# Hybrid diffusion backbone: the scan's decay matrices built in whole rows, and an instruction order taken from the timing simulator

## The chip, the cores and the metric

The kernel runs on one core of a Trainium2 chip. The metric is device time in microseconds (us) of one execution. TensorE (PE) does matmuls and, on a second track (PEld), loads their weights; VectorE (DVE), ScalarE (ACT) and GpSimd (POOL) do the rest; SyncE (SP) and POOL issue most of the transfers (DMA) between memory (HBM) and on-chip SBUF. Every engine takes its own instructions strictly in the order in which the program lists them, and waits on semaphores for the others.

## The reference

Two layers (`DEPTH = 2`) over 256 latent and 256 context tokens of width 1024. A layer is a token mixer with three branches (HGRN2 linear recurrence, grouped-query attention, Mamba-2 SSD), then a SwiGLU network. The last layer computes outputs for latent tokens alone. The change is in the SSD branch: 4 groups of 8 heads, scanned forward and backward in chunks of 128 tokens.

```python
def step(state, blk):                      # ssd_scan, one chunk
    xc, dtc, bc, cc = blk
    acum = jnp.cumsum(dtc * a, axis=1)
    seg = acum[:, :, None, :] - acum[:, None, :, :]
    decay = jnp.exp(jnp.where(causal, seg, -jnp.inf)).reshape(n, L, L, G, HPG)
    xdt = (xc * dtc[..., None]).reshape(n, L, G, HPG, MB_HEAD_DIM)
    cb = jnp.einsum("btgn,bsgn->btsg", cc, bc)
    y = jnp.einsum("btsg,btsgh,bsghp->btghp", cb, decay, xdt)
    ...                                    # plus C against the carried state
```

For each head the kernel needs a matrix over (s, t) of exp(acum_t - acum_s), cut to a triangle, times the step size of s, times C·B. Forward and backward are summed before the matmul.

## The kernel before

**Dense products.** Weights are streamed in pieces of 512 KB by SP (`Weights._load`) into 4 buffers `wraw`. `_split` (L125, L126) makes of each piece a rounded part `wh` on ACT and a remainder `wl` on DVE, with 3 buffers each; a dense product is three matmuls (`mm3`: hh·wh, hl·wh, hh·wl) into a PSUM tile `g`. 48 such matmuls make a unit. The adaLN weights come as "ticks" (`mod_step`): a piece of 512 KB that is not split, read by 8 matmuls `mod` right out of `wraw`, with a tick behind each unit.

**Staging.** Each layer runs the SSD branch, then HGRN2, attention, merge, output projection and feed-forward. `Weave` mixes two generators in the order in which they are recorded: dense units as the main one, the branch's own steps as the side one. In the SSD stage the side one is `ssd_scan` for one group: transposes `xtok`, `Btok`, `cb` = C·B, `state`, and then four pairs of heads. At a layer's start `ssd_tok` transposes the step sizes (`dtT`).

**One head before.** POOL loads the head's cumulated decay row for both directions to all partitions (`ab`, 512 KB) from a DRAM tile `sd`, and e^acum (`ce`, 256 KB) from the same tile. `tk` holds log(dt_s) - acum_s, one number to a partition. DVE makes D = ab + tk + triangle (`neg`) for every 128x128 block and direction; ACT takes exp of D as a whole, and separately exp of the blocks that need no triangle into M; DVE adds the two directions in M and multiplies by `cb`. Then PE does the pair's `y` matmuls from M and from `ce`. In layer 0 a head has both token segments (1024 columns), in layer 1 the latent one alone (512).

**Buffers.** `ab`, D, M, `xt`, `cb`, `state` and others share 10 buffers "b" of 128x1032; 53 buffers "a" of 128x512 hold `ce` and everything else. A load into a buffer waits until the last reader of its old contents is done.

**Order.** Within data dependencies a scheduler in the tile framework sets each engine's order: it plays the recorded program on a model of the machine and issues what is ready there, by priority. Buffers are given out in the same run.

Of the kernel before, what the change touches and what calls it, by code (L numbers as in the profile page):

```python
# [6 lines left out]
F32 = mybir.dt.float32  # L7
F32R = mybir.dt.float32r
I32 = mybir.dt.int32
AF = mybir.ActivationFunctionType  # L10
ALU = mybir.AluOpType
AX = mybir.AxisListType.X

P = 128
# [4 lines left out]
SEQ = 256  # L19
CTX = 256  # L20
T = SEQ + CTX
# [17 lines left out]
def vw(ap, off, dims):  # L39
    return bass.AP(ap.tensor, ap.offset + off, [list(ap.ap[0])] + [list(d) for d in dims])  # L40
# [103 lines left out]
class Net:  # L144
# [468 lines left out]
        yield  # L613


    def ssd_dt_plan(self, l):
        self.w.add(("dt", l), [self.io["w_in"][l][:, O_DT:O_DT + 64].rearrange("(k p) c -> p k c", p=P)])

    def ssd_dt(self, l):

        nc, lay = self.nc, self.lay[l]
        R, N = 64, SEQ
        wh, wl = self.w.take(("dt", l))
        ps = self.pg()
        for k in range(ND):
            self.mm3(ps[0:R, :], wh[:, k], wl[:, k], self.hh[k], self.hl[k], k == 0, k == ND - 1)
        self.act(lay["a"], self.par(l, V_AL), AF.Exp)
        self.ts(lay["a"], lay["a"], -1.0, ALU.mult)
        x, m, y, r, z, p = (self.a(name=n)[:, 0:N] for n in ("dx", "dm", "dy", "dr", "dz", "dp"))
        for sg in range(2):  # L630
            self.ts(x[R * sg:R * sg + R], ps[0:R, N * sg:N * sg + N], self.par(l, V_DTB)[0:R], ALU.add)
        self.ts(m, x, 0.0, ALU.max)
        self.act(y, x, AF.Abs)
        self.act(y, y, AF.Exp, scale=-1.0)
        self.ts(r, y, 2.0, ALU.add)
        nc.vector.reciprocal(out=r, in_=r)
        self.tt(z, y, r, ALU.mult)
        self.tt(z, z, z, ALU.mult)
        self.ts(p, z, 1.0 / 15.0, ALU.mult)
        for c in (13, 11, 9, 7, 5, 3):  # L640
            self.stt(p, p, 1.0 / c, z, ALU.add, ALU.mult)
        self.ts(r, r, 2.0, ALU.mult)
        self.stt(r, p, 1.0, r, ALU.add, ALU.mult)
        dt = z
        self.tt(dt, y, r, ALU.mult)
        self.tt(dt, dt, m, ALU.add)
        self.act(y, m, AF.Exp, scale=-1.0)
        self.tt(y, y, r, ALU.mult)
        self.tt(y, y, m, ALU.add)
        self.act(y, y, AF.Ln)  # L650
        ln = r
        self.stt(ln, x, 0.0, y, ALU.min, ALU.add)
        da, one, s = p, m, x
        self.ts(da, dt, lay["a"], ALU.mult)
        nc.vector.memset(one, 1.0)
        for sg in range(2):
            f, b = slice(R * sg, R * sg + 32), slice(R * sg + 32, R * sg + R)
            nc.vector.tensor_tensor_scan(out=s[f], data0=one[f], data1=da[f], initial=0.0, op0=ALU.mult, op1=ALU.add)
            rv = lambda t: vw(t[b], N - 1, [[-1, N]])
            nc.vector.tensor_tensor_scan(out=rv(s), data0=one[b], data1=rv(da), initial=0.0, op0=ALU.mult, op1=ALU.add)  # L660
        sd = self.dp.tile([R, T + SEQ], F32, name=f"sd{l}")
        for sg in range(2):
            nc.gpsimd.dma_start(out=sd[:, N * sg:N * sg + N], in_=s[R * sg:R * sg + R])
        es = one
        self.act(es[R:P], s[R:P], AF.Exp)
        nc.gpsimd.dma_start(out=sd[:, T:T + SEQ], in_=es[R:P])
        pt = y
        self.tt(pt, ln, s, ALU.subtract)
        we = z
        self.ts(we[0:32], pt[0:32], s[0:32, N - 1:N], ALU.add)  # L670
        self.ts(we[32:R], pt[32:R], s[32:R, 0:1], ALU.add)
        self.last = self.act(we[0:R], we[0:R], AF.Exp)
        return {"sd": sd, "pt": pt, "we": we}
# [89 lines left out]

    def ssd_scan(self, l, g, st, dts, wc, ys):

        nc, lay = self.nc, self.lay[l]
        if "tk" not in dts:
            self.ssd_tok(dts)
        sd, tk = dts["sd"], dts["tk"]
        ts = T + SEQ  # L770
        q0 = 0 if wc else CTX
        segs = (0, 1) if wc else (1,)
        s0, ns = segs[0], len(segs)
        xt, bt = [self.b(name="xt") for _ in range(2)], self.a(name="bt")
        xs = lambda tt, o, n: xt[tt // 2][:, 512 * (tt % 2) + o:512 * (tt % 2) + o + n]
        for tt in range(4):
            ps = self.ps("xtok")
# [4 lines left out]
        ps = self.ps("Btok")  # L782
# [4 lines left out]
        cb = self.b(name="cb")  # L787
        for sg in segs:
            ps = self.ps("cb")
            for s in range(2):  # L790
                c = 256 * sg
                self.mm(ps[:, 256 * s:256 * s + 256], st["B"][:, c + P * s:c + P * s + P], st["C"][:, c:c + 256])
            self.act(cb[:, 512 * sg:512 * sg + 512], ps, AF.Copy)
        yield
        state = self.b(name="state")
        for dr in range(2):
            ps = self.ps("state")
# [7 lines left out]
        for pr in range(4):  # L805
            ms, ce = {}, {}
            for i in range(2):
                h = 8 * g + 2 * pr + i
                ab = self.b(name="ab")
                nc.gpsimd.dma_start(out=ab.rearrange("p (d t) -> p d t", d=2),  # L810
                                    in_=bass.AP(sd.tensor, sd.offset + h * ts, [[0, P], [32 * ts, 2], [1, T]]))
                D, M = self.b(name="D"), self.b(name="M")
                for sg in segs:
                    for s in range(2):
                        tt = 2 * sg + s
                        for dr in range(2):
                            o = 512 * sg + 256 * s + P * dr
                            self.stt(D[:, o:o + P], ab[:, T * dr + P * tt:T * dr + P * tt + P],
                                     tk[:, tt, 32 * dr + h:32 * dr + h + 1], self.neg[:, dr, :], ALU.add, ALU.add)
                        o, a0 = 512 * sg + 256 * s + P * (1 - s), T * s + 256 * sg + P * (1 - s)  # L820
                        self.act(M[:, o:o + P], ab[:, a0:a0 + P], AF.Exp, bias=tk[:, tt, 32 * s + h:32 * s + h + 1])
                dv = D[:, 512 * s0:1024]
                self.last = self.act(dv, dv, AF.Exp)
                o = 512 * s0
                self.tt(vw(M, o, [[512, ns], [256 + P, 2], [1, P]]), vw(D, o, [[512, ns], [256, 2], [1, P]]),
                        vw(D, o + P, [[512, ns], [256, 2], [1, P]]), ALU.add)
                self.tt(M[:, o:1024], M[:, o:1024], cb[:, o:1024], ALU.mult)
                ms[i] = M
                e = self.a(name="ce")
                ev = e.rearrange("p (d t) -> p d t", d=2)  # L830
                nc.gpsimd.dma_start(out=ev, in_=bass.AP(sd.tensor, sd.offset + h * ts + T, [[0, P], [32 * ts, 2], [1, SEQ]]))
                self.tt(ev, ev, vw(st["C"], CTX, [[0, 2], [1, SEQ]]), ALU.mult)
                ce[i] = e
                yield
            yp = self.ps("y")
            for sg in segs:
                ops = [[], []]
                for i in range(2):
                    hc = 64 * (2 * pr + i)
                    ops[i] += [(xs(2 * sg + s, hc, 64), ms[i][:, 512 * sg + 256 * s:512 * sg + 256 * s + 256]) for s in range(2)]  # L840
                    if sg == 1:
                        ops[i] += [(state[:, 512 * dr + hc:512 * dr + hc + 64], ce[i][:, SEQ * dr:SEQ * dr + SEQ]) for dr in range(2)]
                n = len(ops[0])
                for j in range(n):
                    for i in range(2):
                        self.mm(yp[64 * i:64 * i + 64, 256 * sg:256 * sg + 256], *ops[i][j], j == 0, j == n - 1)
            y = self.a(name="y")
            n = 4 * g + pr
            self.stt(y[:, q0:T], st["x"][pr][:, q0:T], self.par(l, V_D + n), yp[:, q0:T], ALU.mult, ALU.add)
            ys.append(y)  # L850
            yield
# [732 lines left out]
```

## Time and profile before

| | us |
|---|---|
| median of 3 runs (lowest, highest) | 2683.18 (2682.48, 2686.78) |
| profiled execution, its own time | 2682.9 |
| its span, first to last instruction | 2681.0 |
| PE busy | 2597.5 (97%) |
| DVE, ACT, POOL busy | 1782.2, 1233.2, 193.0 |
| mean DMA rate | 139 GB/s over the span |

The profiled execution is 0.3 us below the median. PE is busy almost throughout, so the table alone says little: the ends of matmuls are modelled and overlap, a busy PE can run at half clock, and the waits lie in a few stages. The stages of the profiled execution are: the start to 40 us (adaLN weights), layer 0's SSD to 536 us, its HGRN2 to 1206, the rest of layer 0 to 1675, layer 1's SSD to 2010, its HGRN2 to 2300, then attention, merge and feed-forward to the end.

### The profile page before, as it was taken

How to read it: one execution, taken by the hardware profiler on the slowest of the kernel's cores; microseconds unless marked ns; L12 is line 12 of the kernel's file. 1: busy time of each engine (PE TensorE's matmuls, PEld its weight loads, DVE VectorE, ACT ScalarE, POOL GpSimd, SP SyncE). 2: the span in 40 equal slices, each digit the busy share in tenths (PEclk: the TensorE clock that was granted, in tenths of full speed). 3: DMA queues.
4: the chain of work that ended last, by engine and by line, in shares of the span. 5: the costliest groups of instructions: out<-in, count | busy, mean ns of one | idle time of the engine just before them, and what ended most of it. 6: DMA issues, size and time to landing. Idle time of an engine off the chain costs nothing. (4 is left out here: it accounts for less than half of the span.)

```text
span 2681.0 us, 46307 instructions
## 1 busy us (share of the span) xinstructions
PE 2597.5 (97%) x18660; PEld 2139.5 (80%) x18660; DVE 1782.2 (66%) x3708; ACT 1233.2 (46%) x2030; POOL 193.0 (7%) x320
## 2 busy tenths in 40 slices
PE   7999989999999999999999999899999999999999
PEld 4767667788888897777888878677878898888998
DVE  5887776756565575457533358887877777857555
ACT  3655554632333324545432226565654334465543
POOL 0111010000000001010000000111110011111000
PEclk9999999999999999999999999899999999999999
DMA  7566555544444444352333323455763353446553
GB/s 248 147 178 178 147 163 157 150 120 116 118 142 134 123 138 154 94 194 70 102 95 102 95 79 99 132 161 161 222 185 108 98 144 109 140 122 201 166 183 109
DMA packets 298952, 374.41 MB, mean 140 GB/s; under 512 B 16433, under 2 KB 251985, under 8 KB 298737
## 3 DMA queue, kind: packets, MB, share of 16 engines
q1 hardware_dynamic: 271568, 284.21, 35.2%
q0 software_dynamic: 25728, 84.61, 11.1%
q8 instruction: 147, 2.41, 0.4%
q10 hardware_dynamic: 1440, 2.62, 0.3%
q14 instruction: 69, 0.56, 0.1%
HBM read 355.27 MB, written 16.12 MB: 139 GB/s over the span
## 5 line engine op out<-in xcount | busy, mean ns | idle before, releaser
L126 DVE TENSOR_TENSOR wl<-wraw,wh 128x1024 fp32r<-128x1024 f32 (+1 forms) x450 | 544.0, 1211 | 417.1 <-ACT wh L125 408.6
L125 ACT ACTIVATE wh<-wraw 128x1024 fp32r<-128x1024 f32 (+1 forms) x450 | 470.9, 1048 | 699.1 <-PE g L204 509.9
L204 PE MATMUL g<-hh,wh 128*128 128x512 f32 (+2 forms) x2032 | 731.8, 362 | 4.8 <-ACT hh L190 2.2
L204 PE MATMUL g<-hh,wl 128*128 128x512 f32 (+2 forms) x2032 | 723.0, 357 | 5.3 <-DVE wl L126 5.3
L204 PE MATMUL g<-hl,wh 128*128 128x512 f32 (+2 forms) x2032 | 724.6, 357 | 0.0
L204 PEld LDWEIGHTS g<-hh,wh 128*128 128x128 f32 (+1 forms) x2032 | 386.5, 191 | 75.9 <-issue 15.5
L204 PEld LDWEIGHTS g<-hh,wl 128*128 128x128 f32 (+1 forms) x2032 | 386.8, 191 | 68.7 <-issue 9.5
L204 PEld LDWEIGHTS g<-hl,wh 128*128 128x128 f32 (+1 forms) x2032 | 387.4, 191 | 61.8 <-issue 12.9
L204 PE MATMUL g<-oh,wh 128*128 128x512 f32 (+1 forms) x864 | 300.9, 350 | 2.4 <-DVE gl L193 1.3
L204 PE MATMUL g<-ol,wh 128*128 128x512 f32 (+1 forms) x864 | 295.3, 342 | 0.2 <-DVE ol L196 0.2
L204 PE MATMUL g<-oh,wl 128*128 128x512 f32 (+1 forms) x864 | 292.8, 340 | 0.5 <-DVE wl L126 0.5
L204 PE MATMUL g<-wh,hh 128*128 128x256 f32 x768 | 220.7, 287 | 0.0
L204 PE MATMUL g<-wh,hl 128*128 128x256 f32 x768 | 219.2, 285 | 0.0
L204 PE MATMUL g<-wl,hh 128*128 128x256 f32 x768 | 218.1, 284 | 0.0
L204 PEld LDWEIGHTS g<-oh,wh 128*128 128x128 f32 x864 | 163.7, 190 | 29.6 <-issue 7.9
L204 PEld LDWEIGHTS g<-ol,wh 128*128 128x128 f32 x864 | 164.3, 190 | 22.7 <-issue 6.3
L204 PEld LDWEIGHTS g<-oh,wl 128*128 128x128 f32 x864 | 164.0, 190 | 20.2 <-issue 2.7
L204 PEld LDWEIGHTS g<-wh,hh 128*128 128x128 f32 x768 | 147.1, 192 | 3.1 <-issue 2.6
L204 PEld LDWEIGHTS g<-wh,hl 128*128 128x128 f32 x768 | 147.2, 192 | 2.2 <-issue 1.9
L204 PEld LDWEIGHTS g<-wl,hh 128*128 128x128 f32 x768 | 147.2, 192 | 0.5 <-issue 0.4
L196 DVE SCALAR_TENSOR_TENSOR u<-craw,vec,u 128x508 f32<-128x508 f32 (+3 forms) x192 | 130.6, 721 | 8.6 <-ACT u L190 7.6
L196 DVE SCALAR_TENSOR_TENSOR D<-ab,tk,neg 128x128 f32<-128x128 f32 x384 | 110.2, 346 | 22.3 <-DMA ab<-sd 22.1
(303 smaller groups left out, 3577.7 us busy)
## 6 DMA issues: line engine op xcount, KB each, us to landing
wraw<-in_w_in SPq DMA_DIRECT2D x216, 512.0 KB, 4.1
wraw<-in_w_mod SPq DMA_DIRECT2D x96, 512.0 KB, 4.1
wraw<-in_w_ffn_in SPq DMA_DIRECT2D x88, 512.0 KB, 3.5
ab<-sd POOLq DMA_DIRECT2D x64, 512.0 KB, 6.8
wraw<-in_w_ffn_out SPq DMA_DIRECT2D x40, 512.0 KB, 3.4
ce<-sd POOLq DMA_DIRECT2D x64, 256.0 KB, 7.6
wraw<-in_w_br_mb SPq DMA_DIRECT2D x32, 512.0 KB, 3.4
wraw<-in_w_in SPq DMA_DIRECT2D x34, 256.0 KB, 3.6
```

The costliest lines, as they stand in the source:

```text
L125: self.nc.scalar.activation(hi[:, 0:n], t[:, 0:n], AF.Copy)
L126: self.nc.vector.tensor_tensor(out=lo[:, 0:n], in0=t[:, 0:n], in1=hi[:, 0:n], op=ALU.subtract)
L196: return self.nc.vector.scalar_tensor_tensor(out=out, in0=a, scalar=s, in1=b, op0=op0, op1=op1)
L204: return self.nc.tensor.matmul(out, l, r, start=start, stop=stop)
```

## The change

`sd` gets 256 more columns: per direction and segment a copy of the 128 positions whose block needs the other direction's triangle. A head now loads M itself from the decay rows (direction by direction, all positions of its segments), and a small tile E (from the 53 buffers "a") with the other direction's rows of the diagonal blocks. DVE adds the triangles to the diagonal blocks of M in one instruction and to E in another; ACT takes exp in place with `tk` as its per-partition bias (256 columns at a time in M, 128 in E); DVE adds E into M's diagonal blocks and multiplies by `cb`. D and `ab` are gone. `cb` and the `y` matmuls follow M's new layout (s outermost). The scheduler's model is exchanged for the timing simulator by one argument.

```diff
@@ ssd_dt
-        sd = self.dp.tile([R, T + SEQ], F32, name=f"sd{l}")
+        sd = self.dp.tile([R, self.SD], F32, name=f"sd{l}")       # SD = T + SEQ + 2 * P
         for sg in range(2):
             nc.gpsimd.dma_start(out=sd[:, N * sg:N * sg + N], in_=s[R * sg:R * sg + R])
+            for d in range(2):
+                o, r = T + SEQ + P * sg, 32 * d
+                nc.gpsimd.dma_start(out=sd[r:r + 32, o:o + P], in_=s[R * sg + r:R * sg + r + 32, P * (1 - d):P * (1 - d) + P])
@@ ssd_scan, one head
-                ab = self.b(name="ab")
-                nc.gpsimd.dma_start(out=ab.rearrange("p (d t) -> p d t", d=2),
-                                    in_=bass.AP(sd.tensor, sd.offset + h * ts, [[0, P], [32 * ts, 2], [1, T]]))
-                D, M = self.b(name="D"), self.b(name="M")
+                M, E = self.b(name="M"), self.a(name="E")
+                whole = lambda z: vw(z, 256 * s0, [[512, 2], [1, 256 * ns]])
+                diag = vw(M, 256 * s0, [[512 + P, 2], [256, ns], [1, P]])
+                other = vw(E, P * s0, [[256, 2], [P, ns], [1, P]])
+                row = sd.offset + h * ts + 256 * s0
+                nc.gpsimd.dma_start(out=whole(M), in_=bass.AP(sd.tensor, row, [[0, P], [32 * ts, 2], [1, 256 * ns]]))
+                nc.gpsimd.dma_start(out=vw(E, P * s0, [[256, 2], [1, P * ns]]),
+                                    in_=bass.AP(sd.tensor, row + T + SEQ - P * s0, [[0, P], [32 * ts, 2], [1, P * ns]]))
+                for z in (diag, other):
+                    self.tt(z, z, vw(self.neg, 0, [[P, 2], [0, ns], [1, P]]), ALU.add)
                 for sg in segs:
                     for s in range(2):
-                        tt = 2 * sg + s
-                        for dr in range(2):
-                            o = 512 * sg + 256 * s + P * dr
-                            self.stt(D[:, o:o + P], ab[:, T * dr + P * tt:T * dr + P * tt + P],
-                                     tk[:, tt, 32 * dr + h:32 * dr + h + 1], self.neg[:, dr, :], ALU.add, ALU.add)
-                        o, a0 = 512 * sg + 256 * s + P * (1 - s), T * s + 256 * sg + P * (1 - s)
-                        self.act(M[:, o:o + P], ab[:, a0:a0 + P], AF.Exp, bias=tk[:, tt, 32 * s + h:32 * s + h + 1])
-                dv = D[:, 512 * s0:1024]
-                self.last = self.act(dv, dv, AF.Exp)
-                ...
+                        z = M[:, 512 * s + 256 * sg:512 * s + 256 * sg + 256]
+                        self.act(z, z, AF.Exp, bias=tk[:, 2 * sg + s, 32 * s + h:32 * s + h + 1])
+                for sg in segs:
+                    for s in range(2):
+                        z, d = E[:, 256 * (1 - s) + P * sg:256 * (1 - s) + P * sg + P], 1 - s
+                        self.last = self.act(z, z, AF.Exp, bias=tk[:, 2 * sg + s, 32 * d + h:32 * d + h + 1])
+                self.tt(diag, diag, vw(E, 256 + P * s0, [[-256, 2], [P, ns], [1, P]]), ALU.add)
+                self.tt(whole(M), whole(M), whole(cb), ALU.mult)
@@ kernel
-    with tile.TileContext(nc) as tc:
+    with tile.TileContext(nc, schedule_with_timeline_sim=True) as tc:
```

The order of every engine but SP changes throughout. Three places follow; in the rows a number behind the name `sd` is the tile's.

POOL's queue at the third scan of layer 0, before: the loads for two pairs of heads stand first (`ab`; the scan's first two `ce` in the row above them), then pair by pair.

```order
L831 DMA ce<-sd_454 128x2x256 x4
L810 DMA ab<-sd_454 128x2x512 x4
L831 DMA ce<-sd_454 128x2x256 x2
L810 DMA ab<-sd_454 128x2x512 x2
L831 DMA ce<-sd_454 128x2x256 x2
```

The same scan's place in POOL's queue after the change:

```order
L822 DMA E<-sd_454 128x2x256
L839 DMA ce<-sd_454 128x2x256
L822 DMA E<-sd_454 128x2x256
L839 DMA ce<-sd_454 128x2x256
L821 DMA M<-sd_454 128x2x512 x8
L822 DMA E<-sd_454 128x2x256
```

E and `ce` of the first pair come first, then M for all eight heads in one block, then E and `ce` of the second pair and of the others. Six b buffers are free for M. The last two of the eight loads take the buffers of heads 0 and 1 of the same scan, which the first pair's `y` matmuls read; in layer 1 it is the last one.

PE at the third scan of layer 1, before, from the end of the first pair's `y`:

```order
L204 MATMUL g<-hh,wh 128x256
L204 MATMUL y<-M,xt 64x256 x3
L204 MATMUL y<-ce,state 64x256 x4
L204 MATMUL g<-hl,wh 128x256
L204 MATMUL g<-hh,wl 128x256
```

The same place after the change:

```order
L204 MATMUL y<-M,xt 64x256
L204 MATMUL g<-hh,wh 128x256
L204 MATMUL g<-hl,wh 128x256
L204 MATMUL y<-M,xt 64x256 x3
L204 MATMUL y<-ce,state 64x256 x4
L204 MATMUL g<-hh,wl 128x256
```

Before, 22 `g` matmuls follow until the second pair's first `y`; after, 10.

PE at the last pair of layer 0's first scan, before, where the ticks' `mod` matmuls stand one tick at a time:

```order
L204 MATMUL mod<-wraw,sc 32x128 x8
L204 MATMUL g<-hh,wh 128x512
L204 MATMUL g<-hl,wh 128x512
L204 MATMUL g<-hh,wl 128x512
L204 MATMUL g<-hh,wh 128x512
L204 MATMUL y<-M,xt 64x256 x7
L204 MATMUL y<-ce,state 64x256 x4
```

After the change, at the same pair:

```order
L204 MATMUL g<-hh,wl 128x512
L204 MATMUL y<-M,xt 64x256
L204 MATMUL mod<-wraw,sc 32x128 x24
L204 MATMUL y<-M,xt 64x256 x7
L204 MATMUL y<-ce,state 64x256 x4
L204 MATMUL csum<-z,ones_87 32x512 x3
```

Three ticks now stand in one run between two `y` matmuls, with no dense matmul between them.

## Rows read from the trace of the kernel before

**Rows 1.** The page, busy time: engine, us (share of the span) x instructions.

```profile
PE 2597.5 (97%) x18660; PEld 2139.5 (80%) x18660; DVE 1782.2 (66%) x3708; ACT 1233.2 (46%) x2030; POOL 193.0 (7%) x320
```

**Rows 2.** Stretches: length; PE, PEld, DVE, ACT, POOL busy; clock, DMA share, GB/s.

```profile
40.00:536.00 496.00, 480.24 (x2800) 354.50 (x2799) 385.14 (x747) 274.29 (x452) 47.05 (x67) 0.99 0.56 159
1675.00:2010.00 335.00, 308.06 (x1883) 248.51 (x1882) 267.80 (x529) 203.41 (x361) 52.12 (x76) 0.96 0.59 172
```

**Rows 3.** Waits of PE: us in total, times, longest us.

```profile
PE y L204 <- DVE M L193: 25.1, 13, 6.5
PE mod L204 <- DMA wraw<-in_w_mod: 17.8, 15, 5.1
...
PE dtT L208 <- DVE dy L193: 3.0, 1, 3.0
```

**Rows 4.** Timeline around 392 us: start us, us, instruction [idle before <- releaser].

```profile
380.30 0.71 POOL L810 DMA_DIRECT2D ab<-sd  x1 [11.07 <-PE g L204]
...
389.47 1.28 ACT L190 ACTIVATE M<-ab,tk 128x128 f32<-128x128 f32 x4 [5.64 <-DMA ab<-sd]
...
390.81 1.22 DVE L193 TENSOR_TENSOR M<-M,cb 128x1024 f32<-128x1024 f32 x1
...
392.17 1.09 PE L204 MATMUL y<-M,xt 128*64 128x256 f32 x2 [6.50 <-DVE M L193]
```

**Rows 5.** Clock of the core over the span (us, share of full speed).

```profile
core 0: 2681.0 us, clock 0.991
```

**Rows 6.** Three stretches at a low granted clock (columns as in rows 2).

```profile
389.00:396.00 7.00, 3.83 (x9) 2.52 (x10) 6.01 (x14) 3.17 (x6) 0.00 (x0) 0.51 0.28 97
1679.00:1690.00 11.00, 9.90 (x25) 6.86 (x26) 10.95 (x19) 9.32 (x14) 2.51 (x4) 0.53 0.23 37
1727.00:1738.00 11.00, 7.98 (x33) 5.59 (x33) 6.01 (x13) 3.20 (x8) 2.53 (x4) 0.53 0.59 168
```

**Rows 7.** Waits of all engines, the longest of POOL for a scan buffer.

```profile
POOL ab L810 <- ACT M L190: 111.7, 7, 43.2
```

**Rows 8.** Groups by shape, DVE: xcount | busy us, mean ns | idle before.

```profile
L196 DVE SCALAR_TENSOR_TENSOR D<-ab,tk,neg 128x128 f32<-128x128 f32 x384 | 110.2, 346 | 22.3 <-DMA ab<-sd 22.1
L193 DVE TENSOR_TENSOR K<-K,tot 128x512 f32<-128x512 f32 x112 | 76.8, 687 | 4.2 <-ACT kc L190 2.4
...
L193 DVE TENSOR_TENSOR Q<-Q,tot 128x256 f32<-128x256 f32 x56 | 23.7, 422 | 16.0 <-PE small L204 7.5 <-PE atp L204 6.6 <-PE far L204 1.3
```

**Rows 9.** The same for ACT.

```profile
L190 ACT ACTIVATE M<-ab,tk 128x128 f32<-128x128 f32 x192 | 63.3, 391 | 51.5 <-DMA ab<-sd 51.3
...
L190 ACT ACTIVATE D<-D 128x1024 f32<-128x1024 f32 x32 | 33.8, 1056 | 43.4 <-DVE D L196 43.3
...
L190 ACT ACTIVATE kc<-K 128x256 f32<-128x256 f32 x40 | 16.8, 427 | 19.7 <-PE g L204 12.7 <-PE small L204 4.8 <-DVE K L193 1.5
```

**Rows 10.** Issues of transfers: xcount, KB each, median us to landing.

```profile
wraw<-in_w_mod SPq DMA_DIRECT2D x96, 512.0 KB, 4.1
...
ab<-sd POOLq DMA_DIRECT2D x64, 512.0 KB, 6.8
```

**Rows 11.** The tile `ab`, its landing times.

```profile
DMA to landing us min/median/max: 5.0/6.8/12.2
```

**Rows 12.** PE timeline around a narrow side run (columns as in rows 4).

```profile
549.20 0.40 PE L204 MATMUL g<-hh,wh 128*128 128x512 f32 x1
549.53 0.46 PE L204 MATMUL small<-Q,kc 128*32 128x32 f32 x32
549.91 0.50 PE L204 MATMUL g<-hl,wh 128*128 128x512 f32 x1
550.25 0.39 PE L204 MATMUL g<-hh,wl 128*128 128x512 f32 x1
```

**Rows 13.** PE timeline before a side run of full width.

```profile
1698.02 0.39 PE L204 MATMUL g<-hh,wl 128*128 128x512 f32 x1
1698.25 0.38 PE L208 MATMUL xtok<-ident,u 128*128 128x128 f32 x2
```

More of the change, by code (lines that the diff above doesn't have):

```diff
@@ L613, in hgrn_head @@
         yield
+    SD = T + SEQ + 2 * P
     def ssd_dt_plan(self, l):
@@ L769, in ssd_scan @@
         sd, tk = dts["sd"], dts["tk"]
-        ts = T + SEQ
+        ts = self.SD
         q0 = 0 if wc else CTX
@@ L792, in ssd_scan @@
                 self.mm(ps[:, 256 * s:256 * s + 256], st["B"][:, c + P * s:c + P * s + P], st["C"][:, c:c + 256])
-            self.act(cb[:, 512 * sg:512 * sg + 512], ps, AF.Copy)
+            self.act(vw(cb, 256 * sg, [[512, 2], [1, 256]]), vw(ps, 0, [[256, 2], [1, 256]]), AF.Copy)
         yield
@@ L821, in ssd_scan @@
-                        self.act(M[:, o:o + P], ab[:, a0:a0 + P], AF.Exp, bias=tk[:, tt, 32 * s + h:32 * s + h + 1])
-                dv = D[:, 512 * s0:1024]
-                self.last = self.act(dv, dv, AF.Exp)
[L824 to L827, printed above, removed]
+                        z = M[:, 512 * s + 256 * sg:512 * s + 256 * sg + 256]
@@ L839, in ssd_scan @@
                     hc = 64 * (2 * pr + i)
-                    ops[i] += [(xs(2 * sg + s, hc, 64), ms[i][:, 512 * sg + 256 * s:512 * sg + 256 * s + 256]) for s in range(2)]
+                    ops[i] += [(xs(2 * sg + s, hc, 64), ms[i][:, 512 * s + 256 * sg:512 * s + 256 * sg + 256]) for s in range(2)]
                     if sg == 1:
```

## The prediction

> **What bounds the kernel now.** The page's busy times come first: PE is busy 97% of the span [rows 1], and no other engine is near it. Both instruction orders hold the same 15,492 matmuls on PE, so the work itself stays. What can change is 83.5 us of idle PE (2681.0 - 2597.5), time at half clock, and the cost of changing between kinds of matmul. The table by stretch says where the idle time is: 15.8 us in layer 0's SSD stage and 26.9 us in layer 1's [rows 2]; of the rest 17.8 us is `mod` waiting for its first weights [rows 3], nearly all at the start, which the change does not touch, and the remainder are short waits elsewhere. The waits of PE name its cause in the SSD stages: `y` waits for M, 25.1 us in 13 times, the longest kind by far [rows 3]. The timeline around 392 us shows how one comes about. POOL's load of `ab` stood 11.07 us in its queue for a buffer, ACT and DVE then sat until it landed, and `y` came 6.50 us late [rows 4]. POOL's waits say the same in sum: 111.7 us for ACT to be done with a scan buffer [rows 7]. With three buffers to a head out of six, only two heads were under way.
>
> The granted clock is the second loss: 0.991 over the span [rows 5], 24 us of full-speed time. In three stretches it is near 0.5, the 1.2 GHz level, and around each PE had waited (6.5 us for M [rows 4], 3.0 us for `dtT` [rows 3], and at 1727 us for M again); they cost 7 x 0.49 = 3.4, 11 x 0.47 = 5.2 and 5.2 us [rows 6]. Four shorter ones make up the rest.
>
> **The change part by part.**
>
> *The scan's arithmetic.* DVE loses 384 additions into D, 110.2 us, and gains two triangle additions a head. In layer 0 each spans 512 columns (687 ns), in layer 1 256 (422 ns) [rows 8]: 32 x 2 x (0.687 + 0.422) = 71 us, so 39 us less. ACT loses 192 exps of 128 columns (63.3 us, 0.33 each in a row) and those of D (33.8 us in layer 0, by its width an estimated 20 in layer 1), and gains 192 of 256 (0.43, the nearest shape) and 192 of 128: 82 + 63 - 117 = 28 us more [rows 9]. POOL issues 64 loads more at 0.71 us [rows 4], 45 us. None of the three engines sets the end: DVE is the fullest, 268 of 335 us in layer 1's SSD stage [rows 2]. I cost this part at 0; if PE never waited there, DVE with its 268 us, less what it saves, would still be below PE's 308.
>
> *The wait of `y`.* A head now takes one b buffer for its whole life, so six are under way and most loads land long before their use. That takes away the 25.1 us. But POOL's queue has a new place to stand. M of all eight heads is issued in one block; the last two (in layer 1 the last one) wait until the first pair's `y` has read its M, and E of the second pair is queued behind them. From that release the second pair needs: issues of M and E (0.71 each: 2.1 us in layer 0, 1.4 in layer 1), a landing of 6.8 us [rows 10], the triangle on E (0.69 or 0.42), its exps (4 or 2 x 0.33), the sum into M (0.69 or 0.42) and the product with `cb` (1.22 [rows 4]; 0.69 in layer 1): 12.8 us and 10.4 us. PE has until then only what the new order lists between the two pairs. I count it with 0.23 us for a matmul of 512 columns [rows 13], half for 256, and 0.21 for one of `y`: 11.7, 9.5, 15.8, 15.2 us in the four scans of layer 0; 9.4, 5.6, 2.3, 9.7 in layer 1. The third of layer 1 is the piece shown, with 10 matmuls where 22 stood. What is missing is 1.1 + 3.3 + 0 + 0 + 1.0 + 4.8 + 8.1 + 0.7 = 19.0 us. With the shortest landing on record, 5.0, it is 10.8 us; with the longest, 12.2 us [rows 11], 56.8 us. I take the median. Net 19.0 - 25.1 = -6 us, between -14 and +32.
>
> *Layer 1's entry.* `dtT` waited 3.0 us for DVE [rows 3]. In the new order 322 instead of 264 dense matmuls stand between the layer norm's last `spread` and `dtT`, 58 x 0.23 = 13 us more cover. The wait goes, -3 us; next late there are the `xtok` transposes, which wait for the convolutions on DVE. Between -8 and 0.
>
> *Clock.* With that wait its low stretch should go, -5 us. Those behind `y` stay: the waits over 3 us are about as many as before. Between -15 (all of the SSD stages and one more) and +12.
>
> *Fewer changes between dense and side work.* The new order has 387 runs of `g` where 449 stood, 62 fewer, with as many side runs as before (677). One round trip is read off at 549.2 us: the last `g` takes 0.33 instead of 0.23 us, the first one after `small` 0.34, and `small` with 32 columns of width pays about 0.1 on its way out [rows 12, 13]: 0.3 us, so -19 us if each removed run gives it all. But before a side run of full width (`xtok`, 128 columns of the array) the last `g` takes its usual 0.23 us [rows 13]. So the exit costs only where the width changes. I counted width changes over the whole of both orders: 594 before, 587 after. What remains is the slower first `g`, 62 x 0.1 = -6 us, which I take; between -19 and 0. The Trainium skill, page TensorEngine Tiling (Array Packing), section Key Properties, states that changing the tiling mode, as against moving to another tile of the same mode, drains the engine. By that rule the gain is the -6 us, by counting runs alone it would be -19; the two readings of the trace agree with it.
>
> *Ticks in clumps.* `mod` reads its weights out of `wraw`, so a late `mod` holds a buffer. Before, at least 13.9 us of PE work stood between a tick and the first use of what is loaded into its buffer, once the start is over. In the new order four places have less than 5: 2.3, 3.5, 3.9 and 4.7 us, all in layer 0's SSD stage, each time for another tick's weights. Landing takes 4.1 us [rows 10] and the issue some 0.4: 2.2 + 1.0 + 0.6 + 0 = +4 us. If such a load took 12.2 us it would be +34.
>
> *The other short waits of PE.* 83.5 - 17.8 - 25.1 - 3.0 = 38 us are spread over many places. The new order gives dependent small steps more cover: between the three `csum` steps of the SSD norm stand some 24 dense matmuls where 1 to 6 stood, between the levels of HGRN2's `small` 24 to 29 where 4 to 9 did. I take a fifth off, -8 us, between -30 and +20, as every place in the order has changed.
>
> *Sum.* -6 - 3 - 5 - 6 + 4 - 8 = -24 us. The profiled execution took 2682.9 us, 0.3 below the median, so 2659 us for both.
>
> **Rivals.**
>
> *E lands late (slower).* The same block of loads that holds the queue also fills it: 8 x 512 KB of M just ahead of E and beside the weights. For: `ab` already took up to 12.2 us [rows 11], and the stage reads weights at the same time. Against: the first six M are issued a scan's preparation earlier. Price: at 12.2 us the missing time is 56.8 instead of 19.0 us, +38, and a low clock behind each of eight waits of 2 to 14 us at 3.4 us [rows 6], 27 instead of an estimated 12 now, +15. 2659 + 53 = 2712 us. The missing time grows by about 7 us for each us of landing, so it decides against the change from some 10 us on.
>
> *The waits mostly go.* E lands in 5.0 us (-14 instead of -6), the low clock goes from the SSD stages (-15), all round trips count half (-12), the short waits shrink by two thirds (-24), the ticks cost nothing, the entry gives 3: 2683 - 68 = 2615 us. For: each of these places has a simulated latency behind it in the new order, and the csum steps show it. Against: the queue's hold is in the order for all eight scans.
>
> *It changes nothing.* The simulator's order trades waits one for one: the old order also kept PE 97% busy. 2683 us.
>
> **How the numbers follow.** My forecast, 2659 us with 2643 to 2677 as its own range, gets 0.42. The waits mostly go 0.22, E lands late 0.22, no change 0.12; 0.02 is left for something slower still. A measurement of this kernel can tell about 0.2%, 5.4 us, from no change: below 2678 is faster, above 2688.5 slower. The forecast and the second rival give 0.64 for faster, no change with a part of the forecast's edge 0.12, the rest 0.24. The range that holds 8 of 10 cuts the ends of both outer cases: 2612 to 2707 us.
>
> **What would show it.** Right: `y` waiting for M at the second pair of each scan, longest in the third scan of layer 1, with DVE or ACT waiting for E there, and POOL's M load waiting for `y`; no wait of `dtT`; D's row gone from DVE; PE idle below 70 us. Wrong: POOL never held at the seventh or eighth M, or E landing far from 6.8 us; `mod` waiting for `wraw` by more than 10 us past the start; PE's waits in HGRN2 or attention grown, which would say that the simulator's spacing does not fit the chip.

## The result, and the profile after

The changed kernel takes 2858.43 us (median of 4 runs, 2855.13 to 2861.78) where the one before takes 2684.98 (4 runs, 2682.48 to 2687.48): a ratio of 1.065, 95% interval 1.0634 to 1.0667, so 173 us slower. The forecast was 2659 us, range 2612 to 2707. The profiled execution spans 2855.6 us, 174.6 more than before. In one experiment below (PE and DVE held to the old order) one of four executions ran at a mean granted clock of 0.656 and took 3608 us; it is left out of that median.

The page's busy times after, in the form of [rows 1], and the granted clock, as in [rows 5]:

```profile
PE 2641.4 (92%) x18660; PEld 2170.2 (76%) x18660; DVE 1742.2 (61%) x3452; ACT 1258.6 (44%) x2155; POOL 241.4 (8%) x392
```

```profile
core 0: 2855.6 us, clock 0.970
```

PE runs the same 18,660 instructions. Its idle time went from 83.5 to 2855.6 - 2641.4 = 214.2 us, 130.7 more, and it is busy 43.9 us longer, at a mean clock of 0.970 instead of 0.991. The two make up the 174.6 us. The other three engines did what the forecast said: DVE 40 us less, ACT 25 and POOL 48 more.

PE's waits after (us in total, times, longest), for comparison with [rows 3]:

```profile
PE y L204 <- DVE M L193: 50.4, 24, 6.5
PE mod L204 <- DMA wraw<-in_w_mod: 24.6, 21, 5.1
PE spread L204 <- DVE diag L193: 21.6, 7, 3.6
PE oT L208 <- DVE sq L196: 11.6, 5, 3.9
PE dtT L208 <- DVE dy L193: 9.2, 1, 9.2
PE g L204 <- DVE hl L193: 8.1, 4, 3.2
PE g L204 <- ACT wh L125: 8.0, 4, 3.6
PE g L204 <- DVE wl L126: 7.4, 5, 3.5
PE PT L208 <- DVE s L196: 6.9, 3, 3.3
PE PT L208 <- DVE p L200: 6.8, 6, 2.0
```

Four of these kinds before the change:

```profile
PE g L204 <- DVE wl L126: 5.8, 5, 2.3
PE oT L208 <- DVE sq L196: 5.2, 9, 1.8
PE spread L204 <- DVE diag L193: 3.0, 4, 2.5
PE PT L208 <- DVE p L200: 2.3, 2, 1.6
```

The reader is to see two things. The scan's own wait, `y` for M, doubled instead of going away. And below it stands a long list of waits of 2 to 22 us in total for DVE and ACT, most of which were short or absent before; they are the larger part.

Where `y` waits is not where the forecast put it. By pairs of heads, summed over the eight scans, the 50.4 us are about 12.5 at the first pair, 12.6 at the second, 8.6 at the third and 16.6 at the fourth. The second pair is where POOL's queue is held: 7.0 us of its 12.6 lie in the third scan of layer 1, as named, and the other seven scans have 1.2 us or less each. Wherever `y` waits at a third or fourth pair, the pair's M and E had landed 4 to 32 us before DVE's first step on E. The longest such delay stands in layer 0's second scan:

```profile
280.53 0.72 POOL L822 DMA_DIRECT2D E<-sd  x1 [3.72 <-DMA E<-sd]
...
316.94 0.75 DVE L196 SCALAR_TENSOR_TENSOR y<-u,vec,y 128x512 f32<-128x512 f32 x1 [6.39 <-PE y L204]
...
323.55 0.68 DVE L193 TENSOR_TENSOR E<-E,neg 128x512 f32<-128x512 f32 x1
...
328.12 1.22 DVE L193 TENSOR_TENSOR M<-M,cb 128x1024 f32<-128x1024 f32 x1
...
329.40 2.83 PE L204 MATMUL y<-M,xt 128*64 128x256 f32 x12 [5.01 <-DVE M L193]
```

The fourth pair's two E landed by 287.2 us. DVE then sat for 6.39 us at a step that waits for the `y` of the pair before, with the fourth pair behind it in its queue, took up the second of its heads at 323.55, and PE waited 5.01 us for that one. This is the order of DVE, not the transfer.

Where the time went by place: for each stretch of PE's matmuls, its length less the sum of undisturbed steps (for every kind of matmul the 20th percentile of its own step before the change, times their number; where exactly a stretch ends moves a figure by up to 6 us). Dense units may move from one stretch to another in a new order, which this takes out. The last three columns belong to experiments below.

| us above undisturbed steps | before | after | new scan alone | new order alone | after, loads mended |
|---|---|---|---|---|---|
| the two SSD stages | 215 | 295 | 282 | 265 | 248 |
| everything else | 201 | 292 | 199 | 291 | 291 |

The scan touches nothing outside the SSD stages; there the new order costs 90 us by itself. Inside them both cost, and the costs overlap.

POOL's queue and the landings (issues; xcount, KB, median us to landing; M and E of layer 1 have half the size and stand last):

```profile
M<-sd POOLq DMA_DIRECT2D x32, 512.0 KB, 11.3
ce<-sd POOLq DMA_DIRECT2D x64, 256.0 KB, 7.0
...
E<-sd POOLq DMA_DIRECT2D x32, 256.0 KB, 9.0
...
M<-sd POOLq DMA_DIRECT2D x32, 256.0 KB, 7.3
...
E<-sd POOLq DMA_DIRECT2D x32, 128.0 KB, 5.6
```

`ab`, 512 KB in both layers, took 6.8 [rows 10]. So in layer 0 M and E landed later than the 6.8 us of the forecast; in layer 1, where 29 of the 50 us of `y`'s wait lie, E landed sooner.

### The profile page after: what moved, and what is told of

Its sections match the earlier page's. It is cut to its first block, busy times and chain, and to the rows that moved or that the text cites. A ratio compares the mean times of both kernels' runs of the same rounds, so it can differ in the third digit from the quotient of the medians.

```text
span 2855.6 us, 46368 instructions
## 1 busy us (share of the span) xinstructions
PE 2641.4 (92%) x18660; PEld 2170.2 (76%) x18660; DVE 1742.2 (61%) x3452; ACT 1258.6 (44%) x2155; POOL 241.4 (8%) x392
## 5 line engine op out<-in xcount | busy, mean ns | idle before, releaser
L204 PEld LDWEIGHTS g<-hh,wh 128*128 128x128 f32 (+1 forms) x2032 | 388.5, 192 | 99.7 <-issue 13.3
L204 PE MATMUL y<-M,xt 128*64 128x256 f32 x384 | 78.1, 440 | 50.7 <-DVE M L193 50.4
## 6 DMA issues: line engine op xcount, KB each, us to landing
M<-sd POOLq DMA_DIRECT2D x32, 512.0 KB, 11.3
```

The source lines that it names most:

```text
L204: return self.nc.tensor.matmul(out, l, r, start=start, stop=stop)
```

## Experiments

Each kernel ran beside the kernel before on the same chip; given are its median, the difference to before's median there, and the ratio's 95% interval.

**The two halves.** One kernel has the new scan and the old scheduler, the other the old scan and the simulator's order.

```diff
 new scan alone (of the changed kernel)
-    with tile.TileContext(nc, schedule_with_timeline_sim=True) as tc:
+    with tile.TileContext(nc) as tc:
 new order alone (of the kernel before)
-    with tile.TileContext(nc) as tc:
+    with tile.TileContext(nc, schedule_with_timeline_sim=True) as tc:
```

> The new scan (M loaded and finished in place, E beside it) under the old scheduler; nothing of the computation is left out. After against before, PE idles 130 us more and is busy 44 us longer, and by the places of the same steps only 52 of the 175 us lie between the two SSD stages' first and last step. Theory A (the exchange of the scheduler costs it): the old order comes back almost everywhere outside the SSD stages, so the time is near the kernel before, 2670 to 2700 us, and PE's waits other than y stay near 58 us. Theory B (the new scan costs it: M lands in 11.3 us where ab took 6.8, and POOL's queue is held): y still waits some 50 us here, the SSD stages stay some 50 us longer, 2730 us or more. Theory C (only the two together are harmful): 2655 to 2685 us here and in the other half as well.

> The old scan under the order that the timing simulator makes; nothing is left out. Theory A: nearly the whole loss is here, 2800 to 2870 us, with PE idle above 170 us, PE waits of spread, oT, PT and g grown as in the changed kernel, and a granted clock near 0.97. Theory B: 2685 to 2750 us, PE idle below 110 us. Theory C: 2655 to 2685 us.

The new scan alone: 2740.1 us, +58 (1.0187 to 1.0233). The new order alone: 2821.6 us, +139 (1.0507 to 1.0544). Theory A is right for the order (PE idles 166.8 us there, just under the 170 it named) and theory B for the scan; C falls. The sum, 197, is more than the 173 of both, as both lose in the SSD stages.

**The scan: what is held in POOL's queue.** In the new scan alone, third scan of layer 0, POOL's, DVE's and PE's timelines (start us, us, instruction [idle before <- releaser]):

```profile
379.58 1.42 POOL L821 DMA_DIRECT2D M<-sd  x2 [17.57 <-PE y L204]
380.99 0.72 POOL L822 DMA_DIRECT2D E<-sd  x1
...
391.69 0.69 DVE L193 TENSOR_TENSOR E<-E,neg 128x512 f32<-128x512 f32 x1 [1.57 <-DMA E<-sd]
...
395.26 1.22 DVE L193 TENSOR_TENSOR M<-M,cb 128x1024 f32<-128x1024 f32 x1
...
396.63 1.08 PE L204 MATMUL y<-M,xt 128*64 128x256 f32 x2 [5.99 <-DVE M L193]
```

The seventh M load stands 17.57 us for the first pair's `y`; E of the second pair is issued behind it, and DVE gets it 10 us after its issue ended. From the release to the second pair's `y` pass 17 us. The forecast put 12.8 us there, with a landing of 6.8. Such a stall of 5.4 to 6.3 us stands at the second pair of all four scans of layer 0, and with the old order 40 of `y`'s 55.4 us lie at second pairs.

Two ways out: 12 buffers b (and 49 a) so that all eight M fit, with a control on the kernel before; and the loads pinned on POOL in the order M, E, `ce` of one head after another, so that behind a held M only later things stand.

```diff
-        self.n_a, self.n_b, self.n_x = 53, 10, 3
+        self.n_a, self.n_b, self.n_x = 49, 12, 3
 or, for each of the three loads of a head
-                nc.gpsimd.dma_start(out=whole(M), in_=...)
+                self.tc.keep_in_program_order(nc.gpsimd.dma_start(out=whole(M), in_=...))
```

> The new scan under the old scheduler, with 12 buffers b instead of 10 (and 49 buffers a instead of 53, to make room); nothing is left out. Eight M of a group then fit beside xt, cb and state. The scan alone had cost 57 us (2740), with y waiting 55 us for M, once per scan for 6 us at the second pair, where POOL stood at the seventh M load for the first pair's y with E of the second pair behind it. Theory H (the hold in POOL's queue): no M load waits for a y of its own group, y's wait falls under 20 us, and the time to 2680 to 2700 us. Theory L (the loads are just slow: a block of M, E and ce takes 8 to 9 us to land, and M's chain on DVE and ACT is longer): y still waits 40 us or more, 2720 us or more.

> The kernel before with 12 buffers b and 49 buffers a, the control of the run above: it tells what the buffers alone do. If four buffers a less hurt the other stages, 2690 us or more; if ab's own waits for a buffer (111.7 us on POOL, 25.1 us of y's wait) were what the ten buffers cost, 2650 to 2675 us; otherwise 2683 within 5.

> The new scan under the old scheduler with ten buffers b, its loads pinned on POOL in the order M, E, ce of one head after another; nothing is left out. With 12 buffers the hold of the seventh M had gone and 25 of the 57 us with it; y still waited 31 us, and at 92 to 100 us PE idled because six to eight M in a row kept the weights from landing (wh waited 10.3 us for wraw in one piece). Theory Q (what is behind the held M matters): M of head 6 still waits for the first pair's y, but only its own E and ce stand behind it, so y waits at most 30 us and the time is 2695 to 2720 us. Theory D (the burst of loads matters): the wait at 92 to 100 us stays, as six heads are loaded in one go; 2705 us or more. Only if both were unimportant, 2740.

With 12 buffers: 2715.5 us, +32 (1.0101 to 1.0135); `y` waits 31.4 us. The control: 2683.1, no difference (0.9983 to 1.0011). Pinned: 2705.2 us, +22 (1.0074 to 1.0104); `y` waits 19.8 us for DVE's M. The hold is real: without it, or with little behind it, 25 to 36 of the 58 us go, and `y`'s wait at second pairs falls from 40 us to 4.8 (12 buffers; at first pairs it grows from 11 to 22) and 7.9 (pinned). With the buffers the time comes between theories H and L, and eight M at once make the burst below longer; pinned, with ten buffers and the hold still there, it is as theory Q said. This speaks for theory Q, that what stands behind the hold costs more than the hold; but pinning also changes when every other load starts, so it doesn't show it alone.

**The scan: the burst.** At the start of the first scan POOL loads six or eight M at once. Stretches before the change (length; PE, PEld, DVE, ACT, POOL busy; clock, DMA share, GB/s):

```profile
76.00:92.00 16.00, 15.73 (x96) 11.79 (x94) 14.42 (x20) 9.66 (x14) 1.45 (x2) 1.00 0.65 188
92.00:100.00 8.00, 6.17 (x36) 5.05 (x36) 5.86 (x11) 5.50 (x9) 0.00 (x0) 1.00 0.72 215
```

The same with the new scan alone:

```profile
76.00:92.00 16.00, 15.67 (x95) 11.89 (x93) 12.06 (x18) 6.50 (x10) 7.48 (x11) 1.00 0.83 263
92.00:100.00 8.00, 1.67 (x11) 1.18 (x11) 2.41 (x3) 3.15 (x4) 0.00 (x0) 0.75 0.80 275
```

And there, SP's issue of two weight pieces and ACT's first use:

```profile
80.44 2.13 SPq L115 DMA_DIRECT2D wraw<-in_w_in  x2
...
93.75 1.06 ACT L125 ACTIVATE wh<-wraw 128x1024 fp32r<-128x1024 f32 x1 [10.25 <-DMA wraw<-in_w_in]
```

ACT waits 10.25 us for a piece that landed 13.3 us after its issue began (the piece at the same place before the change took 6.9 us; the median of these pieces in this run is 3.9), DVE's weight split and what is queued behind it wait for ACT, and PE does 1.67 us of work in 8. The Trainium skill, page DMA: Bandwidth & Descriptors, section Issuing engines are not separate DMA queues, says that transfers started by different engines run on the same 16 DMA engines and interleave; these rows agree. So the loads were paced: E gets buffers of its own, four (or two), so that a head's loads wait until the E of four (two) heads before is used up.

```diff
-                M, E = self.b(name="M"), self.a(name="E")
+                M, E = self.b(name="M"), self.wp.tile([P, 512], F32, tag="e", name="E", bufs=4)
 (pinned as above, n_a 49; with bufs=2, n_a 51)
```

> The same, with E in four buffers of its own (and 49 buffers a), so that a head's loads start when the E of the head four before it has been added into M: four heads under way instead of six to eight; nothing is left out. Theory D: the weights land as before, PE's wait at 92 to 100 us is below 3 us, wh waits under 28 us for wraw, and the time is 2670 to 2695 us. Theory Q alone: no better than the run before it, or worse by late loads (2705 us or more).

> The new scan under the old scheduler, loads in the order of heads, with E in two buffers of its own (and 51 buffers a): two heads under way, as before the change; nothing is left out. With four it was 2695 us, with PE idle most of 92 to 100 us while 16 loads and the weights shared the queues. Theory D (the burst is what is left): that wait is below 3 us and the time 2675 to 2690 us. Rival: with so few under way y waits for M as in the kernel before or longer (25 us or more): 2695 us or more.

Four: 2695.0 us, +12 (1.0033 to 1.0063), `y` waits 16.0 us. Two: 2707.3, +26 (1.0074 to 1.0112), `y` waits 28.8. Four buffers end at the edge of theory D's range, but its sign at 92 to 100 us did not come: PE still does 1.23 us of work there, and with two buffers 2.82, and `wh` waits 63.9 us in all for these pieces instead of 35.2. Four heads of three loads each are 4 MB, with the pieces beside them still landing in 13 to 17 us; with two the loads come too late for `y`, as the rival said. That the burst delays the weights is shown; that pacing cures it is not. What the four buffers gave, 10 us, lies in layer 1's SSD stage (356 us long, 365 with pinning alone, 357 before the change); the 12 us that are left lie in layer 0's (472 us, 456 before the change).

In the changed kernel the same burst stands there, and weight pieces beside it land in up to 16.1 us, but PE stays busy:

```profile
92.00:100.00 8.00, 8.00 (x42) 6.44 (x41) 4.76 (x10) 7.09 (x13) 4.13 (x6) 1.00 0.93 276
```

So from 92 to 125 us PE does 5.6 us less work than before the change with the new scan alone, and 0.9 us more in the changed kernel: the burst explains nothing of what the changed kernel loses there.

**The order: opening chains by hand.** In the changed kernel PE stands between two steps of the SSD norm with no dense matmul in between:

```profile
210.22 0.95 PE L204 MATMUL csum<-cmb,csum 128*128 128x2 f32 x8
214.72 0.77 PE L204 MATMUL spread<-diag,ones_r 128*128 128x512 f32 x1 [3.56 <-DVE diag L193]
```

In the old order at least 16 dense matmuls stood there, in the new one none in five of the eight SSD norms. Two trials: record a step between and queue `spread` and `oT` behind the dense matmuls recorded before; or give the dense tiles `g` a fourth PSUM bank.

```diff
-        r = self.colrstd(sqs, T - q0, 1.0 / 512, RMS_EPS)
+        v = self.colstat(sqs, T - q0, 1.0 / 512, RMS_EPS)      # colrstd without its spread
         yield
+        with self.tc.issue_after(self.lastg.ins):
+            r = self.spread(v, (T - q0) // P)                   # oT in hgrn_head likewise
+        yield
 the other
-        self.psg = pool("psg", bufs=3, ...); self.pss = pool("pss", bufs=4, ...)
+        self.psg = pool("psg", bufs=4, ...); self.pss = pool("pss", bufs=3, ...)
```

> The old scan under the simulator's order, in which two chains are opened: between the column statistics and the spread matmuls of the SSD norm, and between the HGRN2 norm and its oT transposes, a step is recorded (so that a dense unit is recorded between), and spread and oT are queued on PE behind the dense matmuls recorded before them; nothing is left out. In the simulator's order 0 to 34 dense matmuls stood in the norm's gap, in this one 24 to 87 in all but one place. Theory S1 (PE waits because the new order puts a chain's next PE step right behind the last): spread's 15.6 us and oT's 10.4 us mostly go and the clock's low stretches behind them, 2822 becomes 2785 to 2800 us. Theory S2 (the waits only move: the dense work there would have waited too): the time stays within 10 us of 2822, and waits of g grow by as much.

> The old scan under the simulator's order with four PSUM banks for the dense tiles g and three for the side work, instead of three and four; nothing is left out. Theory P (PE idles because all g banks are held: their readers on ACT and DVE stand behind the chains' small steps): PE's idle time falls from 167 us to below 130, 2770 us or less. Theory S1 (the order itself leaves no dense work in the chains): 2810 to 2840 us, with spread, oT and PT still waiting.

2815.2 and 2818.4 us against 2821.6. S1 fails in the first trial and P in the second. The first comes out as S2 said, within 10 us, and waits of `g` grow (52.0 to 57.4 us): `spread` still waits 13.9 us (4.7 of it at the one place that got no dense work) and `oT` 12.1. What PE waits for at those steps, on DVE, was itself late.

**The order: one engine at a time.** The order of an engine can be imposed: at the end of the recording every instruction of it is queued behind the one that a table, taken from another kernel's program, puts before it. The scheduler is the simulator's in all but the last row of the table below. It still orders the engines that are not held, and it does so around the held ones: by the traces, with PE held only some 60% of DVE's instructions stand in the same sequence as in the new order alone, and with DVE held some 60% of PE's runs of like matmuls. So a row is to be read against the kernel before, and not as the new order less one engine.

```diff
+        for a, b in zip(at, at[1:]):      # at: the order of one engine, from a table
+            tc.add_manual_dep(own[b], own[a].name,
+                              mybir.DependencyInfo(mybir.DependencyClass.NoSync, mybir.DependencyReason.DATA),
+                              reason="order")
```

> The old scan under the simulator's order on ACT, DVE and POOL, but with PE held to the order that the kernel before gave it (each matmul queued behind the one before it in a table); nothing is left out. The simulator's order for all engines takes 2822 us with 167 us of idle PE, the old one 2682. Theory PE (the order of PE is what costs): 2675 to 2715 us. Theory H (the order of the helping engines is what costs, chains standing behind weight splits): 2780 us or more. Between them, both count.

> The mirror image: the old scan under the old scheduler on ACT, DVE and POOL, with PE held to the simulator's order; nothing is left out. Theory PE: 2790 to 2850 us. Theory H: 2720 us or less.

> The old scan under the simulator's order on ACT and POOL alone: PE and DVE are held to the order of the kernel before; nothing is left out. With PE alone held it was 2793 us. Theory V (DVE's order costs: work off the path, as the convolutions, stands between the steps of chains that PE waits for): 2675 to 2705 us. Theory A (ACT's order costs: PSUM banks are freed late, behind the chains' small steps): 2760 us or more.

> The same with PE and ACT held to the old order, DVE and POOL in the simulator's; nothing is left out. Theory V: 2755 to 2800 us, and dtT still waits over 10 us. Theory A: 2675 to 2705 us.

> The old scan under the simulator's order on PE, ACT and POOL, with DVE alone held to the old order; nothing is left out. If DVE's order by itself is the cause: 2690 to 2760 us. If it is that an order must fit the other engines' orders, so that any one held apart costs (as PE held to the simulator's order among the old ones cost 218 us): 2800 us or more.

> The old scan under the simulator's scheduler, with PE, DVE and ACT all held to the order of the kernel before; POOL's queue then differs in a few places alone, and buffers are given out by the simulator's run; nothing is left out. If the 48 us left with PE and DVE held are ACT's order: 2675 to 2692 us. If they are POOL's or the buffers': 2715 us or more.

| old scan, simulator's scheduler; held to the old order | us | to before | 95% interval of the ratio |
|---|---|---|---|
| nothing | 2821.6 | +139 | 1.0507 to 1.0544 |
| PE | 2792.6 | +110 | 1.0376 to 1.0422 |
| PE and ACT | 2768.3 | +87 | 1.0295 to 1.0337 |
| PE and DVE | 2727.6 | +46 | 1.0146 to 1.0200 |
| PE, DVE and ACT | 2681.8 | +1 | 0.9982 to 1.0008 |
| DVE alone | 2888.3 | +207 | 1.0748 to 1.0794 |
| old scheduler, PE held to the simulator's order | 2900.6 | +218 | 1.0792 to 1.0848 |

The last row but two closes the account: with three engines in the old order nothing is left. POOL's queue then has 318 of its 320 instructions in the old sequence, so the buffers that the simulator's run gave out cost nothing; a queue of POOL as different as in the new order alone is not tested beside three old orders. With PE in the very order of the kernel before, 110 us are still lost, so they come from the engines left free: the cover on PE, on which the forecast was built, can't be what decides them. An order of the simulator's on ACT (with nearly the old queue of POOL) loses 46 us beside old orders of PE and DVE, and one on DVE 87 beside old orders of PE and ACT. What PE's new order would cost among the old orders of the others isn't shown: in the bottom row the old scheduler has ordered DVE and ACT anew around it. The two bottom rows show that holding one engine to an order made elsewhere can cost more than the new order as a whole, so the parts are not plain sums. Of the theories, H came true for PE held, and neither PE nor H for the bottom row; V and A both miss with PE and DVE held, as the time lies between them, and V comes true with PE and ACT held; for DVE alone the second came true, and for all three ACT's order.

How DVE's order costs is seen at layer 1's entry. The chain of the step sizes (`dy`, `dx`, `dz`), whose end `dtT` waits for, before the change:

```profile
1672.21 0.42 DVE L193 TENSOR_TENSOR dy<-dy,dr 128x256 f32<-128x256 f32 x1
1672.66 0.42 DVE L193 TENSOR_TENSOR dy<-dy,dm 128x256 f32<-128x256 f32 x1
1673.01 0.74 DVE L196 SCALAR_TENSOR_TENSOR u<-craw,vec,u 128x508 f32<-128x508 f32 x1
...
1676.13 0.67 DVE L658 TENSOR_TENSOR_SCAN dx<-dm,dp 32x256 f32<-32x256 f32 x1
...
1680.61 0.69 DVE L200 TENSOR_SCALAR dz<-dy,dx 32x256 f32<-32x256 f32 x2
```

And after:

```profile
1768.10 0.42 DVE L193 TENSOR_TENSOR dy<-dy,dr 128x256 f32<-128x256 f32 x1
...
1770.22 4.44 DVE L196 SCALAR_TENSOR_TENSOR u<-craw,vec,u 128x510 f32<-128x510 f32 x7
1774.58 0.42 DVE L193 TENSOR_TENSOR dy<-dy,dm 128x256 f32<-128x256 f32 x1
...
1779.16 3.12 DVE L196 SCALAR_TENSOR_TENSOR u<-craw,vec,u 128x510 f32<-128x510 f32 x5
...
1784.54 3.12 DVE L196 SCALAR_TENSOR_TENSOR u<-craw,vec,u 128x508 f32<-128x508 f32 x5
...
1789.37 0.67 DVE L660 TENSOR_TENSOR_SCAN dx<-dm,dp 32x256 f32<-32x256 f32 x1
...
1796.51 0.69 DVE L200 TENSOR_SCALAR dz<-dy,dx 32x256 f32<-32x256 f32 x2
```

From the first step to the last pass 28.4 us instead of 8.4. Before, 4 convolution steps `u` stand within; after, 29 of them and five weight splits `wl`, ahead of chain steps in DVE's queue. This is not all work that could wait: PE itself waits 2.64 us for one of the splits within the chain, and in the new order `xtok`, which reads the convolutions, stands right behind `dtT` on PE. With PE alone held to the old order 18 dense matmuls stand between `dtT` and `xtok`, as before the change, and `xtok` doesn't wait; DVE still has 21 convolution steps within the chain, and `dtT` waits even longer:

```profile
PE dtT L208 <- DVE dy L193: 21.2, 1, 21.2
```

With PE and DVE held it is 7.0 us, with three engines 3.0, as before the change. On ACT the reverse is seen beside the `spread` above, a chain's step ahead of other work: ACT sits 8.23 us at the small step `sr` for DVE's square root, and the copy `craw<-g` that frees a bank of the dense work stands behind it:

```profile
213.57 0.21 ACT L190 ACTIVATE sr<-s 128x4 fp32r<-128x4 f32 x1 [8.23 <-DVE s L196]
213.68 0.58 ACT L190 ACTIVATE craw<-g 128x512 f32<-128x512 f32 x1
```

What this one costs PE isn't shown. Why the simulator prefers such orders (which of its durations is off) none of these runs tells.

**Together.** The changed kernel with the scan's loads pinned and paced, otherwise as it is:

> The changed kernel with the scan's loads in the order of heads and E in four buffers of its own (49 buffers a); nothing is left out. Under the old scheduler this gave back 45 of the new scan's 57 us. If the two halves add, 2805 to 2825 us (2858 less 35 to 50); if the simulator's order had its own cure or cost there, 2840 us or more.

2807.8 us, +127 (1.0446 to 1.0483), 51 us below the changed kernel, nearly all of it in the SSD stages (last column of the table above): the scan's repair holds in the new order, and what remains is the order. PE idles 34.6 us less there, of which `y` for M gives 7.7 (50.4 to 42.7). It is also 12 us faster, each against the kernel before, than the old scan in the new order (+139, intervals apart), while under the old scheduler the same scan is 12 us slower than the old one: which scan is better depends on the scheduler. No kernel here beats the one before.

## Why the prediction was wrong

- *The scan's arithmetic, 0.* Right: DVE -40, ACT +25, POOL +48 us (forecast -39, +28, +45), and none of them sets the end by its load.
- *The wait of `y`, 25.1 to 19.0 us.* Measured: 50.4 us. The term for POOL's hold, 19.0, was not too small: the second pairs waited 12.6 us, most of it in the third scan of layer 1, as forecast. What failed is "That takes away the 25.1 us": the other pairs, put at nothing since their loads land long before, waited 37.7 us. At the third and fourth pairs (25.2 us) the loads had landed, and DVE came late; at the first pairs (12.5 us) both occur. Under the old order second pairs have the larger part, 40 of 55.4 us, and they fall to 4.8 and 7.9 us in the kernels without the hold or with little behind it. The landing, taken from `ab` [rows 10], was also off: in layer 0 M took 11.3 us and E 9.0, in blocks of six M and more. The rival "E lands late" had that, deciding from 10 us on; the new scan alone came to 2740 us, above its 2712, and in the changed kernel it is not what decided.
- *Layer 1's entry, -3.* Wrong: `dtT` waited 9.2 us. I counted 13 us more cover on PE and held the chain on DVE fixed; from its first step shown to its last pass it grew by 20 us. The order of DVE was there to read.
- *Clock, -5.* Wrong: 0.970 instead of 0.991. With 131 us more of waits PE is also 43.9 us longer busy on the same matmuls.
- *Fewer changes, -6.* Can't be seen beside the rest.
- *Ticks in clumps, +4.* The mechanism was right, the size about half: past the start `mod` waits 8.7 us, in six places of layer 0's SSD stage, where it never waited before (in all 24.6 instead of 17.8 us).
- *The other short waits, -8, between -30 and +20.* This step failed most. Idle time without `mod`, `y` and `dtT` went from 37.6 to 130.0 us, +92. It was argued from cover on PE at two kinds of places (the `csum` steps and the levels of `small`), and cover was then carried over to all others. At `spread`, one step behind the `csum` steps, the cover itself went, from at least 16 dense matmuls to none in five of eight norms (3.0 to 21.6 us). Elsewhere the wait is the chain's length less the cover, and the orders of DVE and ACT lengthen the chain: with PE's order unchanged the simulator's orders on the others lose 110 us. The sign that I had named for this, waits in HGRN2 and attention grown, came.

The range was also too narrow by its own logic: it priced a new order of every engine at +20 us at most, with nothing in the trace of before that could bound it. The result lies in the 0.02 that was left for something slower still.

## What to carry to other kernels

When a scheduler changes, read the order of the helping engines as closely as that of the busiest: for each chain that it waits for, count what stands between the chain's steps on DVE and ACT. More of a buffer's life given to one tile lets more loads start at once; price their landing as a burst, and look at what is queued behind the first load that has to wait. An order can be moved to another scheduler one engine at a time; the scheduler orders the free engines anew around it, so compare each such kernel with the one whose order is held.

## What the runs showed of the hardware that was not expected

Ten broadcast loads within 9 us came with a DMA share of 0.83 instead of 0.65, and a weight piece on another engine's queue then took 13.3 us to land, where the piece at the same place took 6.9 before. And more waits came with longer work: each of these three kernels was longer busy on the same matmuls, by 26 us with 39 us more idle time (the new scan alone, mean clock 0.979), 60 with 83 (the new order alone, 0.971) and 44 with 131 (both, 0.970; before 0.991). How much of the longer work is the clock was not taken apart.
